# The MLP's second projection by a seven-product (Strassen) scheme summed in PSUM, and the residual in memory meanwhile

## The chip, the cores and the metric

One core of a Trainium2 chip runs the whole program. The metric is device time in microseconds (us), as the median of several runs. The core has a matrix engine (TensorE, PE in the rows, with PEld for its weight loads), two engines for elementwise work that can read PSUM (VectorE = DVE, ScalarE = ACT), GpSimd (POOL), and SyncE (SP), whose queue issues the DMAs here.

## The reference, cut to what matters

Two decoder layers over 512 tokens of width 1024: a token mixer, a cross-attention and an MLP, each between two RMS norms and added to the residual. The change is in the MLP:

```
for l in range(DEPTH):                       # DEPTH = 2
    a = hybrid_mixer(rms_norm(x, pre_mix_g[l]), ...)
    x = x + rms_norm(a, post_mix_g[l])
    c = memory_cross_attention(rms_norm(x, pre_xattn_g[l]), ...)
    x = x + rms_norm(c, post_xattn_g[l])
    hdn = jnp.square(jax.nn.relu(rms_norm(x, pre_mlp_g[l]) @ w_up[l]))   # [512, 4096]
    x = x + rms_norm(hdn @ w_down[l], post_mlp_g[l])                     # [512, 1024]
```

## The kernel before

**A product is three matmuls.** Every operand is held as two parts, `hi` (the value rounded to the matmul's format) and `lo` (the rest). `mm` (L193 to L200) issues hi x lo, lo x hi and hi x hi into one PSUM tile. A part pair costs a ScalarE copy and a VectorE subtraction: for weights in `load_w` (L150 and L151 for `w_down`, 128x1024 at once; L155 and L160 for weights that are also scaled by a norm's gain, 128x512 at a time), for activations in `split_from` (L164 and L166).

**The MLP of a layer runs in four quarters** (`qd_`), each of 1024 of the 4096 hidden features.

- *Up*: two groups `g` of 512 features. `feat_major` accumulates 4 tiles of 128 features x 512 tokens over 8 blocks of depth (64 products, 192 matmuls for the quarter). `ev_up` evacuates a tile by a ReLU on ScalarE (L946), a square on VectorE (L947) and a split. `pfm` names these PSUM tiles, `hr` the activation, `hh` and `hl` its parts.
- *Down*: for each half `n` of the 1024 output columns, `tok_major` multiplies 8 blocks of 128 features by 4 row tiles `t` of 128 tokens (64 products, 192 matmuls again). `ptm` names the PSUM tiles; `ev_dn` copies them into `acc` (L958, first quarter) or adds them to it (L960).
- In the last quarter `ev_dn` also takes the sum of squares, multiplies by the post-norm's gain (L964) and, with the second half of a row tile, calls `add_post_norm` (L374, L377: the residual `xs` gets the normed output), stores `xs`, and in layer 0 starts the next layer's norm for that row tile (`norm_x`: row statistics, `xn` on GpSimd at L362, transposes `tp` on TensorE at L186, a split into `xth`, `xtl`). With `whole=True` the last half finishes one row tile after the other, 24 matmuls each.

**Buffers.** `un` has 49 units of 128x512 and holds the residual, the accumulators, the hidden parts and, in the token mixer, much else. `wp` has 3 raw weight buffers (`raw`) and 5 each of `hi` and `lo`. PSUM has eight banks: 4 in `psm` (projections), 2 in `pss` (scores) and 2 in `pst` (transposes); the last two stand unused during the MLP. SP's queue issues a weight's DMA (L136) as soon as its `raw` buffer is free.

**Order.** Each engine takes its instructions in one fixed order, which a scheduler derives from the program's order and from when operands and buffers become free. `put_off` delays the transposes of a normed row tile by a fixed amount of matmul work, and `flush` issues those that are due.

Of the kernel before, what the change touches and what calls it, by code (L numbers as in the profile page):

```python
# [44 lines left out]
def block_kernel(ctx: ExitStack, tc, x, mem, positions, rel_bias, w_in, q_norm_g, w_uq, kv_norm_g,  # L45
# [9 lines left out]
    un = ctx.enter_context(tc.tile_pool(name="un", bufs=49))  # L55
# [30 lines left out]
    xsave = dr.tile([S, D], F32, name="xsave")  # L86

# [105 lines left out]
    def mm(ps, lh, ll, rh, rl, first, last):  # L193
# [320 lines left out]
    for l in range(DEPTH):  # L514
# [397 lines left out]
        xo = out_proj_steps(w_xo[l], OTh, OTl, row_bcast(post_xattn_g, l), lambda t: norm_x(xth, xtl, t, "n3"))  # L912
# [22 lines left out]
        gb = row_bcast(post_mlp_g, l)  # L935
        acc = [[None, None] for _ in range(NT)]
        ss = [small("mss", 2) for _ in range(NT)]
        nxh = nxl = None
        for qd_ in range(4):
            if qd_ == 3 and l < DEPTH - 1:  # L940
                nxh, nxl = new_xt()
            hid = []
            for g in range(2):
                def ev_up(m, ps):
                    r = unit("hr")
                    nc.scalar.activation(r, ps, AF.Relu)  # L946
                    nc.vector.tensor_mul(r, r, r)  # L947
                    h = unit("hh", dt=WD)
                    lo = unit("hl", dt=WD) if SPLIT else None
                    split_from(h, lo, r)  # L950
                    hid.append((h, lo))
                feat_major(w_up[l], (qd_ * 2 + g) * 512, 4, NK, G_MLP + 8 * l, xh_f, xl_f, S, ev_up,
                           whole=2 if qd_ == 0 and g == 0 else 0)
            for n in range(2):
                def ev_dn(t, ps, n=n, qd_=qd_):
                    if qd_ == 0:
                        acc[t][n] = unit("acc")
                        nc.vector.tensor_copy(acc[t][n], ps)  # L958
                        return
                    nc.vector.tensor_add(acc[t][n], ps, acc[t][n])  # L960
                    if qd_ < 3:
                        return
                    sumsq(acc[t][n], ss[t][:, n:n + 1], scale=1.0 / 32.0)
                    nc.vector.tensor_mul(acc[t][n], acc[t][n], gb[n])  # L964
                    if n == 1:
                        add_post_norm(acc[t], ss[t], t)
                        if l == DEPTH - 1:
                            store_x(t, out[0])
                        else:
                            store_x(t, xsave)  # L970
                            norm_x(nxh, nxl, t, "n1")
                tok_major(w_down[l], n * 512, 512, 8, None,
                          lambda kk, t: hid[kk][0][:, t * 128:(t + 1) * 128],
                          lambda kk, t: hid[kk][1][:, t * 128:(t + 1) * 128] if SPLIT else None, NT, ev_dn,
                          r0=qd_ * 1024, whole=qd_ == 3 and n == 1)
# [37 lines left out]
```

## Time and profile before

| | |
|---|---|
| median of 3 runs | 1575.46 us (1575.09 to 1577.93) |
| profiled execution | 1576.6 us, span 1574.8 us |
| mean granted TensorE clock | 0.997 of full speed |
| TensorE busy | 1539.8 us (98%), 8023 matmuls |
| VectorE busy | 819.8 us (52%) |
| ScalarE busy | 706.7 us (45%) |
| GpSimd busy | 241.2 us (15%) |
| chain of work that ended last | PE 86%, DVE 6%, issue 3%, DMA 2%, ACT 2%, POOL 1% |

Busy time counts an instruction from start to end; neighbours on an engine overlap a little, so a row's mean duration is longer than the pitch at which such instructions follow each other. The profiled execution's time is 1.8 us more than its span, which begins at the first instruction and ends at the last.

### The profile page before, as it was taken

The numbers are of one execution on the slowest core, as the hardware profiler recorded it, in microseconds if no ns is written. First come the engines' busy times: TensorE is split into PE (matmuls) and PEld (weight loads), VectorE is DVE, ScalarE is ACT, GpSimd is POOL, SyncE is SP. The second block draws the span as 40 slices with busy tenths as digits, with TensorE's granted clock in tenths as the row PEclk, the third lists the DMA queues.
The fourth block names the chain that finished last, engine by engine and source line by source line (L and its number), as shares of the span: only waits on it lengthen the run. The fifth ranks groups of instructions, "written<-read, shape, count | busy, mean of one in ns | idle before, by whom it ended". The sixth has DMA issues, their size and how long they took to land.

```text
span 1574.8 us, 21092 instructions
## 1 busy us (share of the span) xinstructions
PE 1539.8 (98%) x8023; PEld 1295.8 (82%) x8023; DVE 819.8 (52%) x1567; ACT 706.7 (45%) x1414; POOL 241.2 (15%) x433
## 2 busy tenths in 40 slices
PE   7999999999999999999999999999999999999998
PEld 5787787898898888888878877878988988888886
DVE  4665865465464343533564676745455444444344
ACT  4465766355353232423344666735455333333241
POOL 2034621112010000000022365202112000000000
PEclk9999999999999999999999999999999999999999
DMA  5522223522133333233341231253231333332321
GB/s 161 161 89 83 94 68 107 174 95 80 54 96 119 94 101 99 94 94 101 96 131 58 93 107 54 92 192 104 69 94 52 123 96 102 97 94 94 105 83 54
DMA packets 82794, 155.68 MB, mean 99 GB/s; under 512 B 5719, under 2 KB 11525, under 8 KB 82693
## 3 DMA queue, kind: packets, MB, share of 16 engines
q1 hardware_dynamic: 82692, 154.33, 31.3%
q8 instruction: 63, 1.03, 0.3%
q14 instruction: 39, 0.31, 0.1%
HBM read 150.10 MB, written 6.84 MB: 100 GB/s over the span
## 4 chain that ended last, share of the span: by engine, by line
PE 86%; DVE 6%; issue 3%; DMA 2%; ACT 2%; POOL 1%; SPq 0%; DVEq 0%; POOLq 0%; ACTq 0%
PE ptm L198 13%; PE ptm L199 13%; PE ptm L200 13%; PE pfm L199 12%; PE pfm L198 12%; PE pfm L200 12%; PE sp L419 3%; DVE wlo L160 3%; PE op L190 2%; PE ptp L186 2%; DMA tb<-tabw 1%; PE tp L186 1%; PE opx L198 1%; DVE P L423 0%; PE opx L200 0%
## 5 line engine op out<-in xcount | busy, mean ns | idle before, releaser
L155 ACT ACTIVATE whi<-raw,gT 128x512 fp32r<-128x512 f32 (+2 forms) x324 | 210.2, 697 | 265.1 <-PE ptm L200 127.1
L160 DVE SCALAR_TENSOR_TENSOR wlo<-raw,gT,whi 128x512 fp32r<-128x512 f32 (+3 forms) x332 | 231.3, 732 | 186.0 <-ACT whi L155 184.2
L199 PE MATMUL pfm<-xth,wlo 128*128 128x512 f32 (+1 forms) x896 | 322.5, 360 | 0.5
L198 PE MATMUL pfm<-xtl,whi 128*128 128x512 f32 (+1 forms) x896 | 322.2, 360 | 0.0
L200 PE MATMUL pfm<-xth,whi 128*128 128x512 f32 (+1 forms) x896 | 321.5, 359 | 0.0
L151 DVE TENSOR_TENSOR wlo<-raw,whi 128x1024 fp32r<-128x1024 f32 x96 | 117.6, 1225 | 214.3 <-ACT whi L150 211.4
L150 ACT ACTIVATE whi<-raw 128x1024 fp32r<-128x1024 f32 x96 | 101.7, 1060 | 223.3 <-PE ptm L200 116.6
L198 PE MATMUL ptm<-wlo,hh 128*128 128x512 f32 x512 | 199.4, 389 | 0.0
L200 PE MATMUL ptm<-whi,hh 128*128 128x512 f32 x512 | 199.2, 389 | 0.0
L199 PE MATMUL ptm<-whi,hl 128*128 128x512 f32 x512 | 199.2, 389 | 0.0
L199 PEld LDWEIGHTS pfm<-xth,wlo 128*128 128x128 f32 x896 | 169.2, 189 | 26.5 <-DVE wlo L160 1.4
L198 PEld LDWEIGHTS pfm<-xtl,whi 128*128 128x128 f32 x896 | 169.3, 189 | 25.5 <-ACT whi L155 0.5
L200 PEld LDWEIGHTS pfm<-xth,whi 128*128 128x128 f32 x896 | 169.2, 189 | 25.3 <-issue 0.5
L123 POOL TENSOR_TENSOR pnr<-pnm,mhalf 128x1 f32<-128x1 f32 x24 | 15.8, 660 | 858.9 <-DVE pnm L374 858.8
L198 PEld LDWEIGHTS ptm<-wlo,hh 128*128 128x128 f32 x512 | 96.1, 188 | 20.0
L200 PEld LDWEIGHTS ptm<-whi,hh 128*128 128x128 f32 x512 | 96.1, 188 | 19.9
L199 PEld LDWEIGHTS ptm<-whi,hl 128*128 128x128 f32 x512 | 96.1, 188 | 19.8
L427 POOL TENSOR_SCALAR P<-P,rs 128x128 f32<-128x128 f32 (+3 forms) x128 | 72.6, 571 | 140.8 <-DVE rs L426 68.4
L425 ACT ACTIVATE P<-P,nm 128x128 f32<-128x128 f32 (+3 forms) x128 | 71.1, 557 | 26.3 <-DVE nm L423 25.6
L198 PE MATMUL ptm<-wlo,xth 128*128 128x512 f32 (+2 forms) x192 | 68.9, 359 | 1.6 <-ACT xth L164 1.4
L199 PE MATMUL ptm<-whi,xtl 128*128 128x512 f32 (+2 forms) x192 | 67.3, 350 | 0.4 <-DVE xtl L166 0.4
L200 PE MATMUL ptm<-whi,xth 128*128 128x512 f32 (+2 forms) x192 | 66.4, 346 | 0.0
(213 smaller groups left out, 2605.4 us busy)
## 6 DMA issues: line engine op xcount, KB each, us to landing
raw<-in_w_up SPq DMA_DIRECT2D x64, 512.0 KB, 3.6
raw<-in_w_down SPq DMA_DIRECT2D x64, 512.0 KB, 3.4
raw<-in_w_in SPq DMA_DIRECT2D x24, 512.0 KB, 3.7
raw<-in_w_xk SPq DMA_DIRECT2D x16, 512.0 KB, 3.4
raw<-in_w_xv SPq DMA_DIRECT2D x16, 512.0 KB, 3.5
raw<-in_w_mix_out SPq DMA_DIRECT2D x16, 512.0 KB, 4.2
raw<-in_w_xq SPq DMA_DIRECT2D x16, 512.0 KB, 3.3
raw<-in_w_xo SPq DMA_DIRECT2D x16, 512.0 KB, 4.2
```

The lines of the kernel that those rows point to most:

```text
L150: nc.scalar.activation(hi[:, :kts, :width], raw[:, :kts, :width], AF.Copy)
L151: nc.vector.tensor_sub(lo[:, :kts, :width], raw[:, :kts, :width], hi[:, :kts, :width].bitcast(F32))
L155: nc.scalar.activation(cols(hi, k, False), cols(raw, k, True), AF.Copy, scale=g)
L160: nc.vector.scalar_tensor_tensor(lv, rv, g, hv, op0=OP.mult, op1=OP.subtract)
L186: nc.tensor.transpose(out_, in_, ident_)
L190: nc.tensor.matmul(ps, lhsT=lhsT, rhs=rhs, start=start, stop=stop)
L198: nc.tensor.matmul(ps, lhsT=lh, rhs=rl, start=first, stop=False)
L199: nc.tensor.matmul(ps, lhsT=ll, rhs=rh, start=False, stop=False)
L200: nc.tensor.matmul(ps, lhsT=lh, rhs=rh, start=False, stop=last)
L419: nc.tensor.matmul(sp[:, :L], lhsT=q[:, i * 128:(i + 1) * 128], rhs=k[:, :L], start=n == 0, stop=n == len(parts) - 1)
L425: nc.scalar.activation(Pi, Pi, AF.Exp, bias=nm[:, i:i + 1], scale=-1.0, accum_out=rs[:, i:i + 1])
L427: nc.gpsimd.tensor_scalar(Pi, Pi, rs[:, i:i + 1], 1.0, op0=OP.mult, op1=OP.mult)
```

## The change

The second projection of a quarter becomes one level of Strassen's scheme (in Winograd's form). Per group of 512 hidden features the activations are a 2x2 block matrix (two halves of 256 tokens by two halves of 256 features) and the weights another (256 features by 512 columns). Seven products of block sums replace eight products of blocks. Each product, with both groups of the quarter summed in PSUM, is 2 groups x 2 depth blocks x 2 row tiles x 3 = 24 matmuls of 512 columns.

- The products come in the order 1, 5, 6, 2, 7, 3, 4. Products 1, 6, 7 and 4 go on accumulating in one PSUM pair (`wa`, from `pss`), 5 and 3 in another (`wc`, from `pst`), and 2 has one of its own (`we`, from `psm`). After each product the running sums are evacuated, still all on VectorE (L1047 copy, L1049 add): 14 evacuations of 128x512 in a quarter instead of 8.
- `left_forms` makes the seven left operands of a group: four VectorE sums or differences and seven splits of 128x512 (four splits before). The square moves from VectorE to ScalarE.
- `right_form` makes the right operands: of seven, four need a VectorE subtraction of 128x1024 first; each is then split by `parts_w` (seven splits of 128x1024 per group, four before).
- `un` goes from 49 to 39 units and `raw` from 3 to 8 buffers, for the whole program. The residual is written to memory (`xmid`) after the cross-attention and read back in the last quarter, after products 5 and 6, as is the post-norm's gain `gb`.
- In the last quarter `done` is called after products 2, 7, 3 and 4: row tiles 0 and 1 are finished by product 3, row tiles 2 and 3 both by product 4, the last.

```diff
-    un = ctx.enter_context(tc.tile_pool(name="un", bufs=49))
+    un = ctx.enter_context(tc.tile_pool(name="un", bufs=39))
...
+    def raw_w(src, r0, kts, c0, width):
+        raw = wp.tile([128, 2, 512], F32, tag="raw", name="raw", bufs=8)
...
+    def parts_w(raw):
+        hi = wp.tile([128, 2, 512], WD, tag="hi", name="whi")
+        lo = wp.tile([128, 2, 512], WD, tag="lo", name="wlo")
+        nc.scalar.activation(hi, raw, AF.Copy)
+        nc.vector.tensor_sub(lo, raw, hi.bitcast(F32))
+        return hi, lo
...
-        raw = wp.tile([128, 2, 512], F32, tag="raw", name="raw", bufs=3)
+        raw = raw_w(src, r0, kts, c0, width)
...
-        xo = out_proj_steps(w_xo[l], OTh, OTl, row_bcast(post_xattn_g, l), lambda t: norm_x(xth, xtl, t, "n3"))
+        xo = out_proj_steps(w_xo[l], OTh, OTl, row_bcast(post_xattn_g, l), lambda t: (norm_x(xth, xtl, t, "n3"), store_x(t, xmid)))
...
+        def left_forms(F, ra, rb):
+
+            a11, a21 = ra[:, :, 0:256], ra[:, :, 256:512]
+            a12, a22 = rb[:, :, 0:256], rb[:, :, 256:512]
+
+            def part(p, src):
+                h, lo = unit("fh", (128, 2, 256), WD), unit("fl", (128, 2, 256), WD)
+                split_from(h, lo, src)
+                F[p].append((h, lo))
+
+            s1, s2 = unit("s1", (128, 2, 256)), unit("s2", (128, 2, 256))
+            part(1, a11)
+            nc.vector.tensor_add(s1, a21, a22)
+            part(5, s1)
+            nc.vector.tensor_sub(s2, s1, a11)
+            part(6, s2)
+            part(2, a12)
+            nc.vector.tensor_sub(a21, a11, a21)
+            part(7, a21)
+            nc.vector.tensor_sub(a12, a12, s2)
+            part(3, a12)
+            part(4, a22)
+
+        def right_form(p, b):
+
+
+            b11, b12, b21, b22 = b
+            if p == 5:
+                nc.vector.tensor_sub(b11, b12, b11)
+            elif p == 6:
+                nc.vector.tensor_sub(b11, b22, b11)
+            elif p == 7:
+                nc.vector.tensor_sub(b12, b22, b12)
+            elif p == 4:
+                nc.vector.tensor_sub(b11, b21, b11)
+            return parts_w({1: b11, 5: b11, 6: b11, 2: b21, 7: b12, 3: b22, 4: b11}[p])
...
                     nc.scalar.activation(r, ps, AF.Relu)
-                    nc.vector.tensor_mul(r, r, r)
...
+                    nc.scalar.activation(r, r, AF.Square)
...
+            A = [pss.tile([128, 512], F32, tag="s", name="wa") for _ in range(2)]
+            C = [pst.tile([128, 512], F32, tag="t", name="wc") for _ in range(2)]
+            E = [None] * 2
+            for p, ps, first, last, dst in ((1, A, True, False, (0, 0)), (5, C, True, False, (2, 1)),
+                                            (6, A, False, False, (0, 1)), (2, E, True, True, (0, 0)),
+                                            (7, A, False, False, (2, 1)), (3, C, False, True, (0, 1)),
+                                            (4, A, False, True, (2, 0))):
+                if p == 2:
+                    E[:] = [mm_ps("we") for _ in range(2)]
+                for g in range(2):
+                    wh, wl_ = right_form(p, B[g])
+                    fh, fl = F[p][g]
+                    for i in range(2):
+                        for j in range(2):
+                            c = slice(j * 128, (j + 1) * 128)
+                            mm(ps[j], fh[:, i, c], fl[:, i, c], wh[:, i, :], wl_[:, i, :],
+                               first and g + i == 0, g + i == 2, not first)
+                for j in range(2):
+                    t, n = dst[0] + j, dst[1]
                     if acc[t][n] is None:
                         acc[t][n] = unit("acc")
-                        nc.vector.tensor_copy(acc[t][n], ps)
...
+                        nc.vector.tensor_copy(acc[t][n], ps[j])
+                    else:
+                        nc.vector.tensor_add(acc[t][n], ps[j], acc[t][n])
+                    if qd_ == 3 and p in (2, 7, 3, 4):
+                        done(t, n)
+                if qd_ == 3 and p == 5:
+                    gb = row_bcast(post_mlp_g, l)
+                    load_x(0, xmid)
+                    load_x(1, xmid)
+                if qd_ == 3 and p == 6:
+                    load_x(2, xmid)
+                    load_x(3, xmid)
+                flush()
```

**VectorE's order, first quarter of layer 0, about the first evacuations of the second projection.** Names: `wlo` is the low part of a weight, `hl` and `fl` the low part of a hidden activation, `acc` an accumulator, `wa`, `wc` and `we` the PSUM pairs of the change. Before:

```order
L166 TENSOR_TENSOR hl_5010<-hr_5006,hh_5009 128x512
L151 TENSOR_TENSOR wlo_5182<-raw_5179,whi_5181 128x1024
L151 TENSOR_TENSOR wlo_5212<-raw_5209,whi_5211 128x1024
L151 TENSOR_TENSOR wlo_5242<-raw_5239,whi_5241 128x1024
L958 COPY acc_5137<-ptm_5019 128x512
L958 COPY acc_5139<-ptm_5026 128x512
```

Of the change, at the same place (L143 is the weight's low part, L178 a left operand's, L973 the last left form, L988 a right form):

```order
L143 TENSOR_TENSOR wlo_5201<-raw_5062,whi_5200 128x1024
L178 TENSOR_TENSOR fl_5038<-ra_4874,fh_5037 128x512
L973 TENSOR_TENSOR rb_4875<-rb_4875,s2_5017 128x2x256
L143 TENSOR_TENSOR wlo_5220<-raw_5052,whi_5219 128x1024
L178 TENSOR_TENSOR fl_5043<-rb_4875,fh_5042 128x512
L988 TENSOR_TENSOR raw_5058<-raw_5062,raw_5058 128x1024
L178 TENSOR_TENSOR fl_5047<-rb_4875,fh_5046 128x512
L1047 COPY acc_5102<-wa_5066 128x512
L1047 COPY acc_5104<-wa_5067 128x512
L1047 COPY acc_5140<-wc_5068 128x512
L1047 COPY acc_5142<-wc_5069 128x512
L1049 TENSOR_TENSOR acc_5102<-we_5182,acc_5102 128x512
```

The first evacuations of `wa`, on which product 6 waits because it accumulates further in that pair, now stand behind all left forms of the second group and behind right operands of later products. On TensorE this first quarter runs the products as 1, 5, 2, 6, a part of 3, 7, the rest of 3, 4.

**VectorE's order, second quarter of layer 0, the same place.** Of the change:

```order
L178 TENSOR_TENSOR fl_5647<-ra_5502,fh_5646 128x512
L143 TENSOR_TENSOR wlo_5770<-raw_5678,whi_5769 128x1024
L966 TENSOR_TENSOR s1_5644<-ra_5502,rb_5503 128x512
L988 TENSOR_TENSOR raw_5678<-raw_5682,raw_5678 128x1024
L178 TENSOR_TENSOR fl_5652<-s1_5644,fh_5651 128x512
L968 TENSOR_TENSOR s2_5645<-s1_5644,ra_5502 128x512
L971 TENSOR_TENSOR ra_5502<-ra_5502 128x2x256
L1049 TENSOR_TENSOR acc_5102<-wa_5694,acc_5102 128x512
L1049 TENSOR_TENSOR acc_5104<-wa_5695,acc_5104 128x512
L178 TENSOR_TENSOR fl_5657<-s2_5645,fh_5656 128x512
L143 TENSOR_TENSOR wlo_5787<-raw_5686,whi_5786 128x1024
```

Here the evacuation of `wa` stands right behind the forms that products 5 and 7 need, ahead of the other left operands. TensorE runs the seven products in the order of the program in this quarter and the two after it.

**VectorE's order at the end of layer 0.** Before, one row tile ends, with 24 matmuls of the next row tile still to run (L160 splits the next layer's weights):

```order
L960 TENSOR_TENSOR acc_5273<-ptm_7015,acc_5273 128x512
L964 TENSOR_TENSOR acc_5273<-acc_5273,gb_4562 128x512
L374 SCALAR_TENSOR_TENSOR pnm_7058<-mss_4567 128x1
L160 SCALAR_TENSOR_TENSOR wlo_7156<-raw_7153,gT_99,whi_7155 128x512
L377 SCALAR_TENSOR_TENSOR xs_2998<-acc_5141,pnr_7060,xs_2998 128x512
L377 SCALAR_TENSOR_TENSOR xs_3000<-acc_5273,pnr_7060,xs_3000 128x512
```

Of the change, from the evacuation of product 3 (L172 splits the next layer's weights, L387 and L390 are the post-norm):

```order
L1049 TENSOR_TENSOR acc_5178<-wc_6938,acc_5178 128x512
L1049 TENSOR_TENSOR acc_5180<-wc_6939,acc_5180 128x512
L172 SCALAR_TENSOR_TENSOR wlo_7329<-raw_7326,gT_100,whi_7328 128x512
L994 TENSOR_TENSOR acc_5178<-acc_5178,gb_7011 128x512
L387 SCALAR_TENSOR_TENSOR pnm_7186<-mss_4570 128x1
L172 SCALAR_TENSOR_TENSOR wlo_7337<-raw_7334,gT_100,whi_7336 128x512
L390 SCALAR_TENSOR_TENSOR xs_7014<-acc_5102,pnr_7188,xs_7014 128x512
L390 SCALAR_TENSOR_TENSOR xs_7016<-acc_5178,pnr_7188,xs_7016 128x512
L172 SCALAR_TENSOR_TENSOR wlo_7337<-raw_7334,gT_100,whi_7336 128x512
L1049 TENSOR_TENSOR acc_5322<-wa_6936,acc_5322 128x512
L348 SCALAR_TENSOR_TENSOR n1m_7199<-n1ms_7194 128x1
L1049 TENSOR_TENSOR acc_5324<-wa_6937,acc_5324 128x512
```

The row tiles now end in pairs: two at the end of product 3, and two at the end of product 4, after which no matmul of this layer is left.

## Rows read from the trace of the kernel before

**Rows 1.** The page's head and first part: busy time, share of the span, instructions.

```profile
span 1574.8 us, 21092 instructions
...
PE 1539.8 (98%) x8023; PEld 1295.8 (82%) x8023; DVE 819.8 (52%) x1567; ACT 706.7 (45%) x1414; POOL 241.2 (15%) x433
```

**Rows 2.** Busy time by stretch: one down and the next up, layer 0.

```profile
core 0: us, PE busy (x) PEld busy (x) DVE busy (x) ACT busy (x) POOL busy (x), PEclk, DMA share, GB/s
500.60:544.10 43.50, 43.50 (x193) 36.05 (x192) 16.50 (x24) 10.43 (x15) 0.00 (x0) 1.00 0.32 97
544.10:587.70 43.60, 43.60 (x194) 36.10 (x193) 20.05 (x26) 17.64 (x25) 0.00 (x0) 1.00 0.30 97
```

**Rows 3.** Groups over a quarter, 600 to 687 us: count | busy us, mean ns | idle.

```profile
L160 DVE SCALAR_TENSOR_TENSOR wlo<-raw,gT,whi 128x512 fp32r<-128x512 f32 x16 | 11.4, 749 | 24.3 <-ACT whi L155 24.1
...
L151 DVE TENSOR_TENSOR wlo<-raw,whi 128x1024 fp32r<-128x1024 f32 x8 | 9.8, 1225 | 19.5 <-ACT whi L150 19.3
L150 ACT ACTIVATE whi<-raw 128x1024 fp32r<-128x1024 f32 x8 | 8.5, 1058 | 19.2 <-PE pfm L200 9.7 <-PE ptm L200 9.5
L166 DVE TENSOR_TENSOR hl<-hr,hh 128x512 fp32r<-128x512 f32 x8 | 5.5, 690 | 4.2 <-ACT hh L164 4.2
...
L960 DVE TENSOR_TENSOR acc<-ptm,acc 128x512 f32<-128x512 f32 x8 | 5.4, 689 | 2.5 <-PE ptm L200 2.5
```

**Rows 4.** ScalarE's longest wait, 500.6 to 761.8 us: total, times, longest.

```profile
ACT whi L155 <- PE ptm L200: 49.9, 12, 4.4
```

**Rows 5.** Timeline of VectorE where it works without a gap: start, duration.

```profile
576.58 1.23 DVE L151 TENSOR_TENSOR wlo<-raw,whi 128x1024 fp32r<-128x1024 f32 x1
577.72 0.69 DVE L166 TENSOR_TENSOR hl<-hr,hh 128x512 fp32r<-128x512 f32 x1
578.32 0.69 DVE L947 TENSOR_TENSOR hr<-hr 128x512 f32<-128x512 f32 x1
```

**Rows 6.** Timeline from layer 0 to layer 1; in brackets the wait and its releaser.

```profile
776.20 0.69 DVE L960 TENSOR_TENSOR acc<-ptm,acc 128x512 f32<-128x512 f32 x1 [2.10 <-PE ptm L200]
...
778.29 0.15 DVE L374 SCALAR_TENSOR_TENSOR pnm<-mss 128x1 f32<-128x1 f32 x1
...
784.03 0.15 DVE L374 SCALAR_TENSOR_TENSOR pnm<-mss 128x1 f32<-128x1 f32 x1
...
788.37 1.36 POOL L362 TENSOR_SCALAR xn<-xs,n1r 128x512 f32<-128x512 f32 x2
...
799.05 0.66 PE L186 MATMUL tp<-ident,xn 128*128 128x128 f32 x4 [1.58 <-POOL xn L362]
```

**Rows 7.** Timeline at the end of the kernel.

```profile
1567.17 0.39 PE L200 MATMUL ptm<-whi,hh 128*128 128x512 f32 x1
1567.60 0.69 DVE L960 TENSOR_TENSOR acc<-ptm,acc 128x512 f32<-128x512 f32 x1 [1.12 <-PE ptm L200]
...
1570.50 1.42 DVE L377 SCALAR_TENSOR_TENSOR xs<-acc,pnr,xs 128x512 f32<-128x512 f32 x2 [0.66 <-POOL pnr L123]
```

**Rows 8.** TensorE after a gap at the start: the window, then the timeline.

```profile
20.00:40.00 20.00, 17.98 (x78) 14.29 (x78) 6.59 (x12) 5.29 (x12) 3.17 (x5) 0.91 0.19 62
...
28.24 1.77 PE L186 MATMUL tp<-ident,xn 128*128 128x128 f32 x8 [1.78 <-POOL xn L362]
...
31.09 0.63 PE L199 MATMUL ptm<-whi,xtl 128*128 128x512 f32 x1
31.52 0.63 PE L200 MATMUL ptm<-whi,xth 128*128 128x512 f32 x1
```

**Rows 9.** Windows outside the MLP, and the longest wait of SP's queue.

```profile
100.00:200.00 100.00, 94.39 (x581) 79.12 (x581) 70.83 (x217) 66.08 (x173) 51.37 (x106) 0.98 0.28 91
880.00:960.00 80.00, 74.94 (x462) 62.37 (x461) 54.16 (x157) 50.60 (x127) 38.06 (x84) 1.00 0.28 91
...
SPq L136 <- DVE wlo L160: 709.1, 145, 21.5
```

More of the change, by code (lines that the diff above doesn't have):

```diff
@@ L86, in block_kernel @@
     xsave = dr.tile([S, D], F32, name="xsave")
+    xmid = dr.tile([S, D], F32, name="xmid")
     def load_x(t, src=None):
@@ L191, in mm32, with mm @@
         clk[0] += rhs.shape[-1] * 0.00167 * rate
-    def mm(ps, lh, ll, rh, rl, first, last):
+    def mm(ps, lh, ll, rh, rl, first, last, more=False):
         clk[0] += ps.shape[-1] * 0.00126
@@ L197, in mm @@
             return
-        nc.tensor.matmul(ps, lhsT=lh, rhs=rl, start=first, stop=False)
-        nc.tensor.matmul(ps, lhsT=ll, rhs=rh, start=False, stop=False)
-        nc.tensor.matmul(ps, lhsT=lh, rhs=rh, start=False, stop=last)
+        nc.tensor.matmul(ps, lhsT=lh, rhs=rl, start=first, stop=False, skip_group_check=more)
+        nc.tensor.matmul(ps, lhsT=ll, rhs=rh, start=False, stop=False, skip_group_check=more)
+        nc.tensor.matmul(ps, lhsT=lh, rhs=rh, start=False, stop=last, skip_group_check=more)
     def chunks(src, r0, nk, c0, width, gcol, rot=0):
@@ L938, in block_kernel, with done @@
         nxh = nxl = None
+        gb = None
+        def left_forms(F, ra, rb):
[28 more added lines that the diff above has]
+            return parts_w({1: b11, 5: b11, 6: b11, 2: b21, 7: b12, 3: b22, 4: b11}[p])
+        def done(t, n):
+            sumsq(acc[t][n], ss[t][:, n:n + 1], scale=1.0 / 32.0)
+            nc.vector.tensor_mul(acc[t][n], acc[t][n], gb[n])
+            ready_halves[t] += 1
+            if ready_halves[t] < 2:
+                return
+            add_post_norm(acc[t], ss[t], t)
+            if l == DEPTH - 1:
+                store_x(t, out[0])
+            else:
+                store_x(t, xsave)
+                norm_x(nxh, nxl, t, "n1")
+        ready_halves = [0] * NT
         for qd_ in range(4):
@@ L952, in block_kernel @@
                 feat_major(w_up[l], (qd_ * 2 + g) * 512, 4, NK, G_MLP + 8 * l, xh_f, xl_f, S, ev_up,
                            whole=2 if qd_ == 0 and g == 0 else 0)
-            for n in range(2):
-                def ev_dn(t, ps, n=n, qd_=qd_):
-                    if qd_ == 0:
-                        acc[t][n] = unit("acc")
-                        nc.vector.tensor_copy(acc[t][n], ps)
[L959 to L975, printed above, removed]
@@ new lines, in block_kernel @@
+                left_forms(F, ra, rb)
+            B = [[raw_w(w_down[l], qd_ * 1024 + g * 512 + r * 256, 2, n * 512, 512)
+                  for r in range(2) for n in range(2)] for g in range(2)]
+            A = [pss.tile([128, 512], F32, tag="s", name="wa") for _ in range(2)]
[17 more added lines that the diff above has]
+                    t, n = dst[0] + j, dst[1]
+                    if acc[t][n] is None:
+                        acc[t][n] = unit("acc")
+                        nc.vector.tensor_copy(acc[t][n], ps[j])
+                    else:
+                        nc.vector.tensor_add(acc[t][n], ps[j], acc[t][n])
[9 more added lines that the diff above has]
+                flush()
```

17 lines of the change are left out of this document (8 added, 9 removed).

## The prediction, made before the changed kernel was run

> **What bounds the kernel now.** I read the page's first part, then windows over the MLP, then groups by line, waits and the timeline where the change puts new work. TensorE is busy 98% of the span [rows 1]. One down projection and one up projection of a quarter each take 43.5 us with TensorE busy throughout at full granted clock, and the DMA engines at a third [rows 2]. So the MLP is paid by the matmul: 43.5 us for 192 of them is 0.2266 us each. The other engines are far from full there: VectorE 16.5 + 20.05 = 36.5 us of 87.1 and ScalarE 10.43 + 17.64 = 28.1 us [rows 2]. ScalarE's longest wait in the weight copies is for TensorE to free a buffer [rows 4]: the weights are prepared ahead, not just in time.
>
> A change below 0.2% (3.2 us) is about what a measurement of this kernel cannot tell from none.
>
> **1. Matmuls removed.** Each of 2 x 4 quarters loses one product of eight, 24 matmuls of 512 columns: 192 x 0.2266 = **-43.5 us**. A quarter becomes 43.6 + 38.1 = 81.6 us, one product 24 x 0.2266 = 5.44 us.
>
> **2. Does the added elementwise work fit?** VectorE, a quarter, with durations of [rows 3], a sum of two 128x512 taken as the L960 row, a 128x1024 difference as the L151 row:
> - up weights, unchanged: 16 x 0.749 = 12.0
> - left operands: 14 splits and 8 sums x 0.69 = 15.2
> - right splits 14 x 1.225 = 17.2, right differences 8 x 1.225 = 9.8
> - evacuations 14 x 0.69 = 9.7
>
> Together 63.9 of 81.6 us, 27 more than before. ScalarE adds six weight copies at 1.058 [rows 3], six activation copies and eight squares of half that size, each no longer than such a copy: at most 28.1 + 6.3 + 14.8 = 49 us. Both fit on average. In the down part alone it is tight. Its seven products need right operands and evacuations of 36.7 us; those of products 1 and 5 (7.4) can be made in the up part, where VectorE is half idle; the left operands of the second group (11 x 0.69 = 7.6) come after the up's last tile. That leaves 36.9 in 38.1 us. Durations overlap, though: back to back, a 1.23 us split is followed after 1.14 and a 0.69 us one after 0.60 [rows 5], so the real load is about a tenth less. Walking VectorE's order of the change through quarter two with full durations, the evacuation of the running pair is done 2.2 us before product 6 needs it, 2.5 before product 7 and 1.6 before product 4. I take **0** for quarters two to four; the cover is these 1.6 to 2.5 us, and if VectorE falls behind by more, the rest is paid eight times (rival 1). From below nothing is to be gained, TensorE having no gap there.
>
> **3. First quarter of a layer.** There the order puts the first evacuations behind all left forms and behind a right operand that needs a buffer which product 5 frees; behind the waiting evacuations stand those of `wc` and `we` and the next right operands. Counted from the end of the up's first group, products 1, 5, 2 end at 27.2, 32.6 and 38.1; the evacuations of `wa` end at 40.0 with full durations, at 38.3 by pitches [rows 5]. Product 6 then waits 1.9 or 0.2 us; between them I take 1, twice: **+2** (0.4 to 4).
>
> The added evacuations are what speaks against the change here: one takes 0.69 us [rows 3], all on VectorE, their number in a quarter goes from 8 to 14 and TensorE's time for them falls. In the trace of before this does not bind, TensorE having no gap [rows 2]. The Trainium skill's "TensorEngine Tiling (Array Packing)", section "PSUM Bottleneck", says that a faster TensorE leaves PSUM's evacuation as slow as it was, that this may become the bottleneck, and that ScalarE and VectorE should share it; by it rival 1 would come about.
>
> **4. From layer 0 to layer 1.** Before, row tiles finish every 5.44 us, and all but the last is normed and transposed under later matmuls. One tile's way: from `acc` to `pnm` 2.1 us (776.20 to 778.29), from `pnm` to `xn` 5.0 us (784.03 to 788.37 plus half of the pair's 1.36), then transposes (0.66 for four) and a split (0.69), about 1.8: together 8.9 us [rows 6]. After, tiles 0 and 1 start it only 5.44 us before the last matmul, and tiles 2 and 3 at the last matmul. TensorE is then idle for 8.9 - 5.44 = 3.5 us, with two tiles sharing VectorE and GpSimd some 4; tiles 1, 2 and 3 follow at GpSimd's 1.36 us a tile, which I put at 2 us more of short waits. Then the clock: after a wait of 1.78 us at the start of the kernel matmuls came every 0.43 us (31.09 to 31.52) instead of 0.23, with a granted clock of 0.91 over that window, the lower level for part of it [rows 8]; ten such matmuls cost 2 us. Before loses 1.58 us there already [rows 6]. 4 + 2 + 2 - 1.6 = **+6.3** (3, if the tiles of product 3 hide nearly all and the clock holds, to 12, if both pairs come in series).
>
> **5. The tail.** Before, from the last matmul's end (1567.17 + 0.23) to the end of the last `xs` (1570.50 + 1.42) 4.5 us pass [rows 7]. After, two row tiles stand there: VectorE has one more evacuation, gain product and pair of residual sums (0.69 + 0.69 + 1.42 = 2.8), in part in the waits for the other engines; a little for the second tile's GpSimd power on top. I take **+3.3** (2.4 to 5). The output's stores are one row tile more behind it, under 1 us, in that range.
>
> **6. Buffers and the residual's trip.** Eight `raw` buffers let SP issue weights earlier; its longest wait is for VectorE to free one, 709 us in all [rows 9]. TensorE's gaps outside the MLP, where that could pay, are 2.0 us in 20 to 40 [rows 8], 5.6 in 100 to 200 and 5.1 in 880 to 960 [rows 9], filled with waits for norms and softmaxes. Ten units fewer in `un` delay the token mixer's tables and scores, on the same stretches. Store and reload of `xs` (16 transfers of 256 KB a layer) lie under an MLP whose DMA share is 0.3 [rows 2]; on SP's queue the reload stands behind weights that are three products ahead. Ends -6 (half of the gaps) and +6 (as much again); without a row nearer to either, **0**.
>
> **Sum.** -43.5 + 2 + 6.3 + 3.3 = -31.9; 1576.6 - 31.9 = 1544.7 for an execution like the profiled one, which is 1.1 above the median shown. Forecast **1544 us**.
>
> **Rivals.**
> - *1. VectorE late in each quarter, 1562 (14%).* If the right operand of product 5 (2 x 2.45 = 4.9 us) isn't made before the up ends, the down needs 41.8 of 38.1 us at full durations, some 38 to 42 by pitch and duration; half of the 3.7 over and a little for the order, 2.3 x 8 = 18 us. For it: VectorE's 0.69 us adds stand in one fixed queue with the forms. Against: VectorE is half idle in the up [rows 2].
> - *2. Outside the MLP, 1559 (8%).* The 39 units hold back a load or a score and the 5.6 us gap of 100 to 200 [rows 9] doubles in two or three places: +15. Against: the order shows no TensorE instruction moved by more than some 20 places there.
> - *3. The ends hidden and the deeper raw buffers paying, 1534 (12%).* Terms 4 and 5 at their lower bounds (-4), term 6 at -6.
> - *4. A cheaper matmul, 1551 (3%).* If a removed matmul was worth only its weight load, 36.05 / 192 = 0.188 us [rows 2], the saving is 36 and not 43.5. Against: the loads lie under the matmuls, whose own pitch is 0.2266 [rows 2]. The Trainium skill's "TensorE: Matmul & The Clock Gate", section "Back-to-back issue gap", states about 131 ns for sustained matmuls of 512 columns, by which the saving would be an estimated 25 us and the time 1562; the trace does not agree, with 227 ns.
> - *5. Slower: each new right operand made only after the product before, 1656 (5%).* VectorE serves in order, and an evacuation waiting for TensorE stops the difference behind it. If the difference, the copy and the split (1.225 + 1.058 + 1.225 = 3.5 us [rows 3]) start only then, TensorE waits 3.5 us at products 5, 6, 7 and 4 of eight quarters: 32 x 3.5 = 112. It decides from 31.9 / 32 = 1.0 us each. For it: evacuations and forms alternate in the order. Against: the form for product 6 stands there ahead of the evacuation of product 1, so one product's 5.44 us lie between, and five `hi` and `lo` buffers hold two products.
> - *6. All gains eaten, no change (2%).* Only rivals 1 and 2 together.
>
> **How the numbers follow.** The forecast with its own range 1537 to 1552 (bounds of terms 3 to 6 combined, the far ends not all at once) has 56%. The range 1531 to 1564 takes in rivals 1 to 4 and leaves out 5, 6 and the far ends. Faster by over 0.2%: 56 + 14 + 8 + 12 + 3, less a little at their edges, 0.93; same 0.02; slower 0.05.
>
> **What would show it.** Right: 192 matmuls fewer than 8023, a down of 38 us, VectorE busy some 215 us more, in quarters two to four no wait of TensorE for a right operand (`wlo`) or an `acc`; one wait near 1 us before product 6 in the first quarter; a gap of 4 to 6 us with the lower clock between the layers; 7 to 8 us after the last matmul. Wrong: TensorE waiting at each product's start for `wlo` (rival 1 or 5), gaps moved in the token mixer (rival 2), or a down that isn't 38 us without any wait (rival 4).

## The result, and the profile after

| | before | after |
|---|---|---|
| median | 1575.39 us (4 runs, 1575.09 to 1577.93) | 1551.88 us (4 runs, 1549.4 to 1555.59) |
| ratio, 95% interval | | 0.9849 [0.9827, 0.9872] |
| span of the profiled execution | 1574.8 us | 1550.6 us |

The change gives 23.5 us. The forecast was 1544 (31.5 us), with a range of 1531 to 1564; the profiled executions differ by 24.2 us. The head and first part of the page after, which answer to [rows 1]:

```profile
span 1550.6 us, 21224 instructions
...
PE 1504.3 (97%) x7831; PEld 1263.1 (81%) x7831; DVE 993.8 (64%) x1775; ACT 819.0 (53%) x1574; POOL 240.7 (16%) x433
```

The 192 matmuls are gone (8023 to 7831), but TensorE's busy time fell by 35.5 us, not by 43.5, and its idle time (span less busy) rose from 35.0 to 46.3. Both are leads: the first says that some matmuls got longer, the second that there are new waits. VectorE is busy 174 us more, less than the forecast's 215: durations overlap where the engine has no gap, and busy time counts that once (a quarter below has 25.48 + 33.09 = 58.6 us where 63.9 were summed).

First the MLP itself: the up and the down of layer 0's second quarter after, as [rows 2], and what TensorE waited for from the first to the last matmul of layer 0's MLP (total, times, longest).

```profile
528.45:572.00 43.55, 43.55 (x194) 36.04 (x193) 25.48 (x32) 21.71 (x34) 0.00 (x0) 1.00 0.20 62
572.00:610.10 38.10, 38.10 (x170) 31.55 (x169) 33.09 (x44) 20.67 (x27) 0.00 (x0) 1.00 0.47 146
```

```profile
PE wa L211 <- DVE acc L1047: 0.3, 1, 0.3
```

A down is 38.1 us with TensorE busy throughout, and the only wait of the four quarters is 0.3 us before product 6 of the first. Layer 1's MLP has the same single wait. VectorE is busy 33.09 of a down's 38.10 us.

So the rest is outside. Windows between the same two matmuls (the first score of the dilated heads and the first of the latent ones), layer 0 then layer 1, of the kernel before:

```profile
88.40:170.80 82.40, 78.04 (x489) 67.32 (x487) 56.05 (x171) 55.17 (x140) 37.76 (x78) 0.98 0.33 102
863.60:945.00 81.40, 76.32 (x489) 65.90 (x487) 54.06 (x167) 51.35 (x133) 36.95 (x78) 1.00 0.33 106
```

and of the changed kernel:

```profile
86.50:172.80 86.30, 79.92 (x490) 67.22 (x488) 52.88 (x167) 53.01 (x134) 37.23 (x78) 0.98 0.32 104
851.20:939.40 88.20, 80.52 (x490) 70.29 (x488) 54.24 (x167) 51.30 (x133) 37.51 (x78) 0.94 0.33 106
```

The same matmuls take 3.9 us more in layer 0 (2.0 idle, 1.9 as longer matmuls) and 6.8 more in layer 1 (2.6 idle, 4.2 as longer matmuls). What TensorE waits for in layer 0 is seen where the first dilated scores stand, by the timelines of ScalarE, VectorE and TensorE after:

```profile
97.43 3.15 ACT L167 ACTIVATE whi<-raw,gT 128x384 fp32r<-128x384 f32 x6 [8.49 <-issue]
100.59 1.28 ACT L438 ACT_TABLE_LOAD   x1
101.89 0.40 ACT L438 ACTIVATE P<-P,nm 128x128 f32<-128x128 f32 x1
```

```profile
98.08 1.15 DVE L172 SCALAR_TENSOR_TENSOR wlo<-raw,gT,whi 128x384 fp32r<-128x384 f32 x2 [8.28 <-ACT whi L167]
```

```profile
101.56 0.49 PE L432 MATMUL sp<-kh,qs 128*128 128x384 f32 x1 [1.86 <-DVE nm L436]
```

ScalarE stands still for 8.49 us ahead of six weight copies, and the first exponentials come behind them. VectorE waits 8.28 us for these copies, with the work on the scores (`nm`) behind. "issue" names no releaser; what it waited for is inferred below. The granted clock right after, in windows of 4 us:

```profile
99.00:103.00 4.00, 2.14 (x10) 1.38 (x8) 3.94 (x13) 3.85 (x9) 0.00 (x0) 0.85 0.69 216
103.00:107.00 4.00, 3.12 (x13) 1.89 (x12) 2.03 (x9) 3.67 (x10) 2.08 (x4) 0.72 0.87 306
```

**The layers' border** is read from the start of the last `pfm` matmul of layer 0 to that of the first of layer 1, as windows, before and then after:

```profile
748.57:820.04 71.47, 69.81 (x322) 57.45 (x321) 42.14 (x67) 32.08 (x65) 13.89 (x16) 1.00 0.33 98
```

```profile
734.97:807.65 72.68, 67.06 (x298) 53.76 (x297) 57.09 (x87) 41.02 (x76) 13.09 (x16) 0.98 0.47 158
```

The waits of the four row tiles' transposes in it, after (they answer to the last of [rows 6]):

```profile
777.13 1.78 PE L198 MATMUL tp<-ident,xn 128*128 128x128 f32 x8 [3.70 <-POOL xn L375]
784.33 1.32 PE L198 MATMUL tp<-ident,xn 128*128 128x128 f32 x8 [0.58 <-POOL xn L375]
790.43 1.32 PE L198 MATMUL tp<-ident,xn 128*128 128x128 f32 x8 [0.91 <-POOL xn L375]
796.26 1.32 PE L198 MATMUL tp<-ident,xn 128*128 128x128 f32 x8 [0.40 <-POOL xn L375]
```

71.47 us before, 72.68 after with a product less: 1.21 + 5.44 = 6.7 us lost, of which 4.0 are idle time (72.68 - 67.06 against 71.47 - 69.81). In the tail, which answers to [rows 7], the last matmul's end (1539.76 + 0.23) to the last `xs` (1546.26 + 1.41 = 1547.67) is 7.7 us instead of 4.5:

```profile
1539.76 0.39 PE L213 MATMUL wa<-whi,fh 128*128 128x512 f32 x1
1540.84 1.28 DVE L1049 TENSOR_TENSOR acc<-wa,acc 128x512 f32<-128x512 f32 x2
...
1546.26 1.41 DVE L390 SCALAR_TENSOR_TENSOR xs<-acc,pnr,xs 128x512 f32<-128x512 f32 x2 [0.66 <-POOL pnr L124]
```

### The profile page after: what moved, and what is told of

It reads as the page before. It is cut to its first block, busy times and chain, and to the rows that moved or that the text cites. A ratio compares the mean times of both kernels' runs of the same rounds, so it can differ in the third digit from the quotient of the medians.

```text
span 1550.6 us, 21224 instructions
## 1 busy us (share of the span) xinstructions
PE 1504.3 (97%) x7831; PEld 1263.1 (81%) x7831; DVE 993.8 (64%) x1775; ACT 819.0 (53%) x1574; POOL 240.7 (16%) x433
## 4 chain that ended last, share of the span: by engine, by line
PE 83%; DVE 7%; issue 4%; ACT 2%; POOL 2%; DMA 2%; SPq 0%; DVEq 0%; POOLq 0%; ACTq 0%
PE pfm L212 12%; PE pfm L211 12%; PE pfm L213 12%; PE ptm L211 6%; PE ptm L212 6%; PE ptm L213 6%; PE wa L211 3%; PE wa L212 3%; PE wa L213 3%; PE sp L432 3%; PE op L202 3%; DVE wlo L172 2%; PE ptp L198 2%; PE wc L211 2%; PE wc L212 2%
## 5 line engine op out<-in xcount | busy, mean ns | idle before, releaser
L172 DVE SCALAR_TENSOR_TENSOR wlo<-raw,gT,whi 128x512 fp32r<-128x512 f32 (+3 forms) x332 | 229.5, 731 | 132.7 <-ACT whi L167 131.1
L142 ACT ACTIVATE whi<-raw 128x1024 fp32r<-128x1024 f32 x112 | 118.9, 1061 | 139.8 <-PE pfm L213 52.8
L143 DVE TENSOR_TENSOR wlo<-raw,whi 128x1024 fp32r<-128x1024 f32 x112 | 134.8, 1220 | 32.0 <-ACT whi L142 32.0
L211 PE MATMUL wa<-wlo,fh 128*128 128x512 f32 x256 | 99.8, 390 | 0.5 <-DVE acc L1047 0.5
L212 PE MATMUL wa<-whi,fl 128*128 128x512 f32 x256 | 99.6, 389 | 0.0
L213 PE MATMUL wa<-whi,fh 128*128 128x512 f32 x256 | 99.6, 389 | 0.0
L163 DVE TENSOR_TENSOR wlo<-raw,whi 128x1024 fp32r<-128x1024 f32 x32 | 39.1, 1223 | 59.3 <-ACT whi L162 58.6
L162 ACT ACTIVATE whi<-raw 128x1024 fp32r<-128x1024 f32 x32 | 34.0, 1061 | 67.3 <-PE ptm L213 64.5
L211 PEld LDWEIGHTS wa<-wlo,fh 128*128 128x128 f32 x256 | 48.0, 188 | 11.3 <-DVE acc L1047 1.4
```

The costliest lines, as they stand in the source:

```text
L142: nc.scalar.activation(hi, raw, AF.Copy)
L143: nc.vector.tensor_sub(lo, raw, hi.bitcast(F32))
L163: nc.vector.tensor_sub(lo[:, :kts, :width], raw[:, :kts, :width], hi[:, :kts, :width].bitcast(F32))
L172: nc.vector.scalar_tensor_tensor(lv, rv, g, hv, op0=OP.mult, op1=OP.subtract)
```

## The experiments

Each ratio is to the kernel before on the same chip in the same session (medians of before there 1575.0 to 1576.7).

### What slows the token mixers: e1, e2, e3, e5, e11

Three parts of the change reach outside the MLP: fewer units, deeper raw buffers, the residual's trip.

**e1**, the kernel before with fewer units:

```diff
-    un = ctx.enter_context(tc.tile_pool(name="un", bufs=49))
+    un = ctx.enter_context(tc.tile_pool(name="un", bufs=39))
```

> The kernel before with un at 39 units and nothing else (raw stays at 3). The order of the weight and table loads on SP's queue is that of the kernel before. Theory R (the deep raw buffers put weight loads ahead of the bias tables on SP's queue): no change, 1575, the dilated scores of head 1 at their old place. Theory U (too few units hold back the tables): the 8 us that the changed kernel lost in its two token mixers, 1583.

Measured 1578.33, ratio 1.0010 [0.9995, 1.0025]. Its two windows are 84.6 and 83.9 us long (before 82.4 and 81.4), with the waits as before and a clock of 0.96 in both; theory U's 8 us aren't there.

**e2**, the same with `raw` at 8:

```diff
-        raw = wp.tile([128, 2, 512], F32, tag="raw", name="raw", bufs=3)
+        raw = wp.tile([128, 2, 512], F32, tag="raw", name="raw", bufs=8)
```

> The kernel before with un at 39 and raw at 8 buffers, the old MLP. SP's queue now has six loads of w_uq and w_ukv ahead of head 1's table, as in the changed kernel. Theories R and U both: 1575 + 8 = 1583, with TensorE's waits of about 2 us before the scores and the lower clock behind them; with e1 the two part. If the loss comes from the new MLP or the residual's trip instead: 1575.

Measured 1580.88, ratio 1.0022 [1.0005, 1.0038]: 3.5 us, less than half of what was expected. Its trace says why. Layer 0 shows the changed kernel's stall with the old MLP, ScalarE's stop and TensorE's wait alike:

```profile
97.23 3.15 ACT L155 ACTIVATE whi<-raw,gT 128x384 fp32r<-128x384 f32 x6 [8.48 <-issue]
```

```profile
101.36 0.44 PE L419 MATMUL sp<-kh,qs 128*128 128x384 f32 x1 [1.86 <-DVE nm L423]
```

and its window is 89.2 us, 6.8 more than before. Layer 1's is 81.2, nothing lost. About 2 us come back ahead of the window, which starts at 86.20 instead of 88.40. So the depth, with e1's units, makes the loss of layer 0; that of layer 1 was not seen without the new MLP.

**e3**, the changed kernel with the bias tables on another queue:

```diff
-            nc.sync.dma_start(tb, bass.AP(...))
+            nc.gpsimd.dma_start(tb, bass.AP(...))
```

> The changed kernel with the bias tables loaded by GpSimd's queue, no longer behind weights on SP's. Theory R: the tables are there early, the mixers lose nothing, 1552 - 8 = 1544. Theory U: the tables still wait for units, 1552. A rival: GpSimd issues late, behind its own score work, or the issuing costs it more than SP, then 1550 to 1556.

Measured 1555.28, ratio 0.9858 [0.9844, 0.9873], no gain on 0.9849. In layer 0 theory R, with the tables on SP's queue as the way, falls: with the tables on another queue ScalarE's stop is just as long,

```profile
95.93 3.15 ACT L167 ACTIVATE whi<-raw,gT 128x384 fp32r<-128x384 f32 x6 [8.49 <-issue]
```

and VectorE's 8.28 us above are a wait for ScalarE, not for a table. In layer 1 theory R is open. There VectorE does wait for tables (`tb`) ahead of the scores, longer in the changed kernel than before; over layer 1's window, before, in the changed kernel and in e3 (total, times, longest):

```profile
DVE P L423 <- DMA tb<-tabw: 4.5, 4, 3.6
```

```profile
DVE P L436 <- DMA tb<-tabw: 8.9, 3, 4.1
```

```profile
DVE P L436 <- DMA tb<-tabw: 11.0, 5, 3.4
```

On GpSimd's queue the tables were late too, which fits the rival that e3's expectation named, so e3 doesn't test the theory there. For layer 0 the trace points at the order of ScalarE and VectorE instead: with eight raw buffers the next weights arrive early, their splits are put ahead of the scores, and in the trace they stand there until 97.43. This is theory S, tested by **e5**, the changed kernel with the eight buffers in two sets, of which five serve the second projection alone:

```diff
-    def raw_w(src, r0, kts, c0, width):
-        raw = wp.tile([128, 2, 512], F32, tag="raw", name="raw", bufs=8)
+    def raw_w(src, r0, kts, c0, width, own=False):
+        raw = wp.tile([128, 2, 512], F32, tag="rawm" if own else "raw", name="raw", bufs=5 if own else 3)
...
-            B = [[raw_w(w_down[l], qd_ * 1024 + g * 512 + r * 256, 2, n * 512, 512)
-                  for r in range(2) for n in range(2)] for g in range(2)]
+            B = [[raw_w(w_down[l], qd_ * 1024 + g * 512 + r * 256, 2, n * 512, 512,
+                        own=n == 0 or (g, r) == (1, 1)) for r in range(2) for n in range(2)] for g in range(2)]
```

> The changed kernel, its eight raw buffers in two sets: three for all weights as before, five more for the second projection alone. Theory S (with eight buffers later weights arrive early, their splits are put ahead of the first scores in the orders of ScalarE and VectorE, and wait there for a hi or lo buffer): the mixers run as before, 6 to 8 us less than the changed kernel's 0.985 of before, ratio 0.980 to 0.981, some 1545. Theory U (39 units): no change, 0.985. Theory C (only the clock's chance): as often above as below 0.985.

Measured 1546.74, ratio 0.9813 [0.9792, 0.9833], span 1542.4: as expected, though the interval just touches the changed kernel's (e9 below, with the same buffers, has 0.9801). The two windows of above, and ScalarE's timeline at the first scores:

```profile
85.80:168.80 83.00, 78.39 (x490) 67.49 (x488) 56.09 (x171) 55.32 (x140) 37.70 (x78) 0.98 0.33 101
847.60:931.40 83.80, 76.58 (x490) 66.01 (x488) 54.20 (x167) 51.44 (x133) 36.99 (x78) 1.00 0.32 103
```

```profile
89.83 1.28 ACT L438 ACT_TABLE_LOAD   x1
91.12 0.40 ACT L438 ACTIVATE P<-P,nm 128x128 f32<-128x128 f32 x1
...
94.17 0.60 ACT L167 ACTIVATE whi<-raw,gT 128x384 fp32r<-128x384 f32 x1
```

The exponentials start at 91.12 instead of 101.89, and the copies of the 384-column weights now stand behind the first of them, from 94.17 on. That these copies had waited for a `hi` or `lo` buffer is argued from this; no row names the buffer. Of the 3.9 and 6.8 us, 0.6 and 2.4 stay.

For layer 0 the profiles of all runs agree. With eight buffers for all weights (the change, e2, e3, e4, e7, e8, e12) its window is 86.3 to 91.2 us long, 5.6 to 8.3 of them idle; with three for the weights outside the second projection (before, e1, e5, e6, e9, e10, e11) it is 81.7 to 84.6 us, 4.4 to 4.8 of them idle.

For layer 1 the buffers aren't shown to be the cause. Of the 4.4 us by which e5's window is shorter only 0.5 are idle time; the rest is the clock, 1.00 instead of 0.94, and e6 below, with e5's buffers, has 87.9 us at 0.94 there. So theory C, chance, stays open for that part. The idle time of layer 1, 5.1 us before and 7.7 in the change, is still 7.2 in e5, and VectorE still waits 6.0 us for tables there.

**e11**, the kernel before with the residual's trip:

```diff
-... lambda t: norm_x(xth, xtl, t, "n3"))
+... lambda t: (norm_x(xth, xtl, t, "n3"), store_x(t, xmid)))
...
+            if qd_ == 3:
+                for t in range(NT):
+                    load_x(t, xmid)
```

> The kernel before with the residual's trip alone: stored after the cross-attention, read back before the last down projection. Forecast's term 6: it lies under the MLP, 1.000 of before. Rival: the store or the reload holds back weights on SP's queue at the MLP's start or in its last quarter: 2 to 4 us more, 1.002.

Measured 1575.23, ratio 1.0002 [0.9990, 1.0014]. The trip costs nothing that can be told from zero, some 2 us at most.

### How much cover VectorE has: e7, e12, e8

**e7** computes the low part of each left operand twice, **e12** for the first group only (the line with `if` then stands above it):

```diff
                 split_from(h, lo, src)
+                nc.vector.tensor_sub(lo, src, h.bitcast(F32))     # e7
...
+                if not F[p]:                                      # e12
+                    nc.vector.tensor_sub(lo, src, h.bitcast(F32))
```

> The changed kernel with the low part of each left operand computed twice: 14 x 0.69 = 9.7 us more for VectorE in a quarter, 73.6 of 81.6 us. Tells how large the cover over VectorE is. If it is some 2 us in each product as the walk gave: 0 to 3 us a quarter are lost, about 8 in all, 1560. If VectorE has room everywhere: 1552. If it was at its edge already: 8 x 6 = 48 more, 1600.

> As e7, but the low parts are computed twice for the first group of a quarter only (7 x 0.69 = 4.8 us a quarter, made while the second up projection runs). If VectorE is at its edge in the down part only: nothing is lost, 0.985 as the changed kernel. If its sum over the whole quarter counts: half of e7's loss, 0.998.

e7 measured 1596.02, ratio 1.0119 [1.0098, 1.0141]: 42 us more than the changed kernel's ratio gives, where 8 were expected. e12 measured 1554.55, ratio 0.9863 [0.9841, 0.9884]: nothing beyond the intervals, against the changed kernel's 0.9849. So of e7's 9.7 us a quarter, the half made during the up costs nothing, and with the half made in the down some 5 us a quarter are lost. What TensorE waited for in e7's layer 0 MLP, and the second quarter's wait:

```profile
PE wa L211 <- DVE wlo L143: 11.3, 3, 3.8
PE wa L211 <- DVE acc L1048: 2.9, 2, 2.8
```

```profile
596.14 0.70 PE L211 MATMUL wa<-wlo,fh 128*128 128x512 f32 x1 [3.76 <-DVE wlo L143]
```

7 x 0.60 = 4.2 us were added to the down by pitch, and one wait of 3.76 us came out, in the middle of product 6 for the split of its second group's right operand. This doesn't measure the room in the changed kernel's own order, because the added work also changed VectorE's order. In the changed kernel, as in e12, that split stands right behind the left operand of product 6:

```profile
579.90 0.68 DVE L178 TENSOR_TENSOR fl<-s,fh 128x512 fp32r<-128x512 f32 x1
580.50 1.22 DVE L143 TENSOR_TENSOR wlo<-raw,whi 128x1024 fp32r<-128x1024 f32 x1
```

In e7 it stands behind the evacuations of `wc` and all left operands of the second group:

```profile
592.98 0.68 DVE L1050 TENSOR_TENSOR acc<-wc,acc 128x512 f32<-128x512 f32 x1
...
594.18 0.68 DVE L178 TENSOR_TENSOR fl<-rb,fh 128x512 fp32r<-128x512 f32 x1
594.78 1.22 DVE L143 TENSOR_TENSOR wlo<-raw,whi 128x1024 fp32r<-128x1024 f32 x1
```

In the changed kernel it is done at 581.72, 3.9 us before the second half of product 6 starts (572.00 + 2.5 x 5.44 = 585.60). In e7 twelve more instructions, 7.2 us by pitch, stand between the split for the first group (581.08) and this one: five second passes, 3.0 us, and seven that stand behind it in the changed kernel, 4.2 us. What 4.2 us of work would cost in the old order no run shows. The longer matmul behind that wait (0.70 instead of 0.39) and the window's clock, 0.96 from 576 to 617, add the rest.

**e8** gives the right operands' differences to GpSimd, idle in the MLP:

```diff
         def right_form(p, b):
...
-                nc.vector.tensor_sub(b11, b12, b11)
+                nc.gpsimd.tensor_sub(b11, b12, b11)     # and so for products 6, 7 and 4
```

> The changed kernel with the differences of the right operands computed by GpSimd, which is idle in the MLP, in all quarters: 9.8 us a quarter off VectorE. If VectorE's load at the border is what delays the row tiles: 2 to 4 us less, 1549. If GpSimd is too slow for two differences in a product's 5.4 us, or the two engines slow each other: TensorE waits in each quarter, 1565 or more.

Measured 1608.73, ratio 1.0199 [1.0178, 1.0220]. Groups by line in e8 (mean ns before the second bar):

```profile
L983 POOL TENSOR_TENSOR raw<-raw 128x1024 f32<-128x1024 f32 x16 | 51.2, 3202 | 403.3 <-DVE wlo L143 403.3
L178 DVE TENSOR_TENSOR fl<-ra,fh 128x512 fp32r<-128x512 f32 x32 | 42.3, 1322 | 44.4 <-ACT fh L176 44.4
```

A difference that took VectorE 1.22 us takes GpSimd 2.7 to 3.2 on average, and VectorE's own 0.69 us splits of `ra` average 1.32 (all 112 left operands 1.04). The Trainium skill's "GPSIMD Engine Reference" (section "Key points") says that GpSimd shares its SBUF interfaces with VectorE and contends with VectorE instructions of two SBUF inputs, such as these splits; the trace agrees, with 1.32 for 0.69. The rival held, though the largest of TensorE's waits is for the left operands that VectorE splits late; how much of this is the slower work and how much another order on VectorE, no run separates (total, times, longest):

```profile
PE wc L212 <- DVE fl L178: 22.0, 8, 2.8
```

### The border and the tail: e4, e6, e9, e10

**e4** and **e6** run product 3 ahead of 7 in the last quarter, and product 4 one row tile after the other; e6, on top of e5, also lets GpSimd multiply by the gain and calls `flush` within the products.

```diff
+            if qd_ == 3:                                   # e4, e6
+                seq[4], seq[5] = seq[5], seq[4]
...
+                rows = [[0], [1]] if qd_ == 3 and p == 4 else [[0, 1]]    # e4, e6, e9
...
-            nc.vector.tensor_mul(acc[t][n], acc[t][n], gb[n])    # e6; left out in e10
+            nc.gpsimd.tensor_mul(acc[t][n], acc[t][n], gb[n])
```

> The changed kernel with another order in the last quarter alone: product 3 ahead of product 7, so that row tiles 0 and 1 end two products before the end, and product 4 one row tile after the other. If the layers' border and the tail cost what the late pairs make them cost: the border gives back some 5 us of its 6.7 and the tail 2 to 3 of its 3, 1552 - 7.5 = 1544. If the border costs because tiles 2 and 3 are late whatever comes before: 1549 at best.

> As e5, and the last quarter as in e4 with two more edits there: the gain's product by GpSimd instead of VectorE, and the transposes of a normed row tile issued within the products. Theory V (at the layers' border VectorE is full, so the row tiles of e4 came late whatever TensorE's order): with 5.5 us taken off VectorE the earlier pair counts, border 3 to 5 and tail 2 to 3 us less than e5: 1538. Rival: the border is set by the last pair's chain of 9 us alone: 2 us for the tail, 1543. Rival: GpSimd's product is slow and makes the chain longer: 1547.

Measured 1555.03, ratio 0.9857 [0.9842, 0.9872] for e4, and 1552.48, 0.9847 [0.9831, 0.9864] for e6: both miss, e6 even loses on e5. TensorE in e6's last quarter:

```profile
1535.19 0.50 PE L211 MATMUL wa<-wlo,fh 128*128 128x512 f32 x1 [3.32 <-DVE acc L1059]
```

With 3 ahead of 7, the post-norm of row tiles 0 and 1, with its waits for ScalarE and GpSimd, stands on VectorE ahead of the evacuation of `wa` after product 7, and product 4 can't start. In the order of the change that evacuation comes first. The gain's products took GpSimd 1.54 us each on average (0.69 on VectorE). Of the 9.8 us by which e6's profile is longer than e5's, 4.1 lie in layer 1's mixer at the lower clock, which the edit doesn't touch.

**e9** is e5 with product 4 row by row and nothing else; **e10** is e5 without the gain's product.

> As e5, and in the last quarter product 4 runs one row tile after the other (12 matmuls each); the order of the products stays, and the gain's product stays with VectorE. Row tile 2 ends 2.7 us earlier. If the tail is the two row tiles standing at one moment: tail 2 us less and the border 0 to 2 us less than e5, ratio 0.9795, some 1544. If VectorE is still busy with row tiles 0 and 1 then, so that nothing starts earlier: as e5, 0.981.

> As e5, but the post-norm's gain product of the MLP is left out (the output then lacks that gain): 5.5 us less for VectorE in each layer's last quarter, nothing else. Theory V (VectorE, full in the last quarter, sets when the row tiles of product 3 are ready): border 2 to 4 us shorter, and the tail by the two products in its chain, 1.4; 0.978, some 1542. Rival (the chain through ScalarE and GpSimd sets it): only the products in the chain count, 1.4 us a layer, 0.9795.

e9: 1544.63, ratio 0.9801 [0.9782, 0.9821]; the last matmul's start to the last `xs` in its timeline:

```profile
1529.27 0.39 PE L213 MATMUL wa<-whi,fh 128*128 128x512 f32 x1
...
1534.52 1.42 DVE L390 SCALAR_TENSOR_TENSOR xs<-acc,pnr,xs 128x512 f32<-128x512 f32 x2 [0.66 <-POOL pnr L124]
```

6.4 us from the last matmul's end (1529.27 + 0.23) to 1535.94, 1.3 less than the changed kernel; the border, 72.5 us against e5's 73.0, hardly changes. e9 is the fastest complete version that was run; its step on e5 is within the intervals, and only the tail's rows show it. e10: 1541.51, ratio 0.9787 [0.9770, 0.9803]. Its border (731.83 to 803.04, read as above) is 71.2 us against e5's 73.0 (731.13 to 804.10), 1.8 less; in the tail, 2.0 less. Theory V expected 2 to 4 at the border, its rival 1.4: VectorE's load counts for a little, the chain of the last row tiles for most.

## Why the prediction was right, and which term was not

The forecast missed by 8 us inside its range, just within the 1537 to 1552 that it gave itself without rivals, and the profiles put nearly all of it on one term. Forecast and measured (profiled executions):

| term | forecast | measured | from |
|---|---|---|---|
| 1 matmuls | -43.5 | -43.5 | 192 fewer, a down of 38.1 us |
| 2 quarters two to four | 0 | 0 | no wait |
| 3 first quarters | +2 | +0.5 | waits of 0.25 and 0.26 |
| 4 border | +6.3 | +6.7 | 1.21 + 5.44 |
| 5 tail | +3.3 | +3.2 | 7.7 - 4.5 |
| 6 buffers, the rest | 0 | +8.9 | what remains of 24.2 |

- **Term 6 is the step that failed.** It weighed "Eight `raw` buffers let SP issue weights earlier" as gain or nothing, and looked at TensorE's order, which moves little there. What moves is ScalarE's and VectorE's order: splits of later weights go ahead of the scores. The two mixer windows lose 3.9 + 6.8 us, of which 1.9 come back at the start (the first dilated score at 86.50 instead of 88.40); 8.9 lies outside the ends of -6 and +6 that the term was given. In e5 the windows are 3.3 + 4.4 us shorter again, and the ratio is 0.9813 instead of 0.9849. The 3.3 are the buffers' doing, as layer 0's windows in all runs show; of the 4.4 only 0.5 are idle time. What makes layer 1 idle 2.6 us longer than before is open: late tables have a part, and the lower clock there comes and goes with the same buffers. Rival 2 named the place (8%, +15) and the wrong part: it blamed the units, which e1 clears of the larger part.
- **Terms 1 and 5 held, and term 4 in its sum.** The border's idle time grew by 4.0 us (4 + 2 - 1.6 = 4.4 was forecast) and its matmuls by 2.7 (2). Inside the wait of 3.70 two errors cancel, which is luck. From the first evacuation of product 3 to the transposes a row tile took 9.6 us (767.53 to 777.13), where the forecast's steps up to there give 2.1 + 5.0 = 7.1, GpSimd's first pair of `xn` with 2.95 instead of 1.36 among the causes; and the 1.8 us that it added for transposes and split are no idle time of TensorE. e10 fits this chain.

```profile
767.53 1.28 DVE L1049 TENSOR_TENSOR acc<-wc,acc 128x512 f32<-128x512 f32 x2
```

```profile
774.80 2.95 POOL L375 TENSOR_SCALAR xn<-xs,n1r 128x512 f32<-128x512 f32 x2
```

- **Term 2 held, with more cover than its text says.** The cover was put at 2.2, 2.5 and 1.6 us for the evacuations of the running pair ahead of products 6, 7 and 4. In the second quarter they end 2.9, 4.4 and 3.5 us before these start (at 572.00 + 2, 4 and 6 x 5.44), since they follow each other by pitch and not by full durations:

```profile
578.70 1.28 DVE L1049 TENSOR_TENSOR acc<-wa,acc 128x512 f32<-128x512 f32 x2
...
588.11 1.28 DVE L1049 TENSOR_TENSOR acc<-wa,acc 128x512 f32<-128x512 f32 x2
...
600.46 0.68 DVE L1049 TENSOR_TENSOR acc<-wa,acc 128x512 f32<-128x512 f32 x1
```

  The right operand of product 6's second group had 3.9 us. Rival 1 (VectorE late in each quarter) is what e7 brought about, by more work and another order together.
- **"PSUM Bottleneck"** of the Trainium skill's "TensorEngine Tiling (Array Packing)", on which the prediction drew, did not bind: no evacuation made TensorE wait in the MLP but for 0.3 us in each first quarter.

## What to carry to other kernels

A seven-product scheme is paid in the elementwise engines, and the room there is read ahead of each product that waits for them, not from a busy share: VectorE showed 33.09 of 38.10 us busy in a down, and the operands and evacuations read here were done 2.9 to 4.4 us early. An edit that adds work can move the order as well, so the order is compared before its cost is called the cost of the work (e7). A buffer pool that one stage needs deeper should be deepened for that stage alone; prefetch elsewhere changes the order of the in-order engines, and work that can't run yet stands ahead of work that could (layer 0). When a pair of late results is to be taken earlier, ask what the same engine must still do for the next product.

## What the runs showed of the hardware

- A wait of some 2 us on TensorE can be followed by a loss of about the same size: around the 1.86 us wait at 101.56, and behind it with TensorE busy 3.12 of 4 us, the granted clock was 0.85 and 0.72 in two windows of 4 us, the lower of the two levels (1.2 instead of 2.4 GHz) for part of each. It isn't certain: the kernel before has such a wait of 1.96 us, and its granted clock is 1.00 in the windows of 4 us from 894 to 902; e5 has one of 2.66 us at 882.00 in a window with 1.00. Longer matmuls make 6.1 of the 10.7 us that the two mixers lose, and the four runs of the change go with the clock, from 1549.4 us at 0.994 to 1555.6 at 0.988.
- GpSimd's 128x1024 difference took 2.7 to 3.2 us on average beside a working VectorE, whose 128x512 splits of the left operands then took 1.04 us on average instead of 0.69, those of `ra` 1.32 (e8).
